# A hybrid block of pooling, gated delta rule and latent attention: four places of the projections' side work

## The chip, the cores and the metric

The kernel runs on one core of one Trainium2 chip. The metric is the device time of one execution in microseconds: the median of three runs of the kernel before is 1230.45 us (1230.11 to 1233.87).

## The reference

One transformer block in float32, 1024 tokens of width 1024. `x` is normalised and projected; the projection is split into a pooling mixer, a gated delta rule (4 heads of 128, chunks) and an attention with latents; their outputs are projected, added to `x`, and a squared-ReLU MLP (1024 to 4096 to 1024) follows.

```python
proj = rms_norm(x, attn_norm) @ w_in
xa, qkv, z, b, a, c_q, c_kv, k_pe = split(proj)
y_a = pool_mixer(xa, ...)                  # windows 2, 4, 8, 16
y_b = gated_deltanet(qkv, z, b, a, ...)    # below
y_c = mla_attention(c_q, c_kv, k_pe, ...)  # latents c_q, c_kv: norm, up-projection, rope, causal softmax
x = x + concat(y_a, y_b, y_c) @ w_out
x = x + square(relu(rms_norm(x, mlp_norm) @ w_up)) @ w_down

# gated_deltanet, per head
q, k, v = split(silu(causal_dwconv(qkv, conv_w)))   # 4 taps
q, k = l2_normalize(q) * D ** -0.5, l2_normalize(k)
a_strict = strict_lower((k * beta) @ k.T * decay)
u, w = solve(I + a_strict, [v * beta, k * beta * exp(gcum)])
attn = lower(q @ k.T * decay)
# scan over the chunks: v_new = u - w @ state; o = q_dec @ state + attn @ v_new;
#                       state = state * g_last + k_dec.T @ v_new
o = rms_norm(o, norm_gain) * silu(z)
```

## The kernel before, in words

Every large product is done in three passes of matmuls on operands split into a high and a low part (`split`, lines 114 to 116: a copy on ScalarE and a subtraction on VectorE or GpSimd; `mm3`, lines 122 to 125). The input projection is made tile by tile: a tile is 128 output channels, and a half tile is 512 tokens of it, 24 matmuls of 512 columns. `proj_tile` (line 479) runs the two halves of one tile. For each half it issues the 24 matmuls into one PSUM bank of the kind `mm` (four of them), calls `use` on the result, then calls what an earlier half tile has left in the list `later`, then `pump(n, m)`, which takes `m` steps of the generators in the queue `slow`, up to two of `ahead` and `n` of those in `side`. After the first half it calls `between`, if there is one.

The order of the tiles is: four key tiles (one per head), two gates, then per head a query tile and a value tile, after the second head two tiles of the pooling mixer, and at the end the other two gates. `conv_silu` (line 498) is the `use` of keys, queries and values: the four taps, the first on ScalarE (line 503), three on VectorE (line 506, reading the PSUM bank, with small pieces on line 508), a Tanh on ScalarE (line 512) and one more VectorE operation (line 514) that stores `kt`, `qt` or a scratch tile. The gates' `use` is a Tanh on ScalarE and the VectorE operation of line 715 that stores `zs`.

Side work that hangs on these tiles:

- `latents()` (line 373), in the queue `slow`: per token tile three steps (`latent_a`: transposes of the latents, up-projection by matmuls, squares), and per pair of token tiles `latent_b` (a Newton iteration of small VectorE operations) and two steps of `latent_c` (fifteen GpSimd operations, one ScalarE operation, a DMA to `n_dram`, line 369). That is 8 steps a pair, 32 for the eight token tiles. During the key tiles `m` is `LAT`, 4; during the gates it is 2.
- For each key head, after its tile: transposes of the keys (line 524), their square sums on ScalarE (line 541), products of the keys with themselves (line 562) and `at` (line 565, VectorE), which goes to `a_dram` (line 566, issued by SyncE) and is read back in another order into `lanes` (line 569).
- After the four key heads: the key scales, a Newton iteration of eleven VectorE operations on 128x32 and one product (lines 576 and 577). They are read on line 705 alone, in `turn_v`.
- `lanes()` (line 580), in the queue `side`: the inverse of 32x32 triangles, one per partition, by 31 steps of two VectorE operations (lines 589 and 591), then a copy of the inverse with its two inner dimensions turned, `TLT` (line 593, VectorE), and two DMAs to `t_dram`: `TL` issued by SyncE, `TLT` by ScalarE.
- `query_key(h)` (line 674): 8 transposes of the query tile, its square sums on ScalarE, 8 products with the keys, and 8 VectorE operations that turn the decay mask `E[h]` into the attention inside a chunk. It is called as `between` of the value tile of the same head, that is behind its first half.
- `turn_v` (line 699): transposes of a half value tile and their scaling; it is left in `later` by one half tile and called behind the matmuls of the next.
- `heads(0, 1)` and `heads(2, 3)` (line 847), in the queue `side`: what builds the whole inverse out of `t_dram` and `a_dram` (`levels`), and the scan over the chunks (`chain`). They begin after the second and after the last head's values.

The order of the instructions on each engine isn't that of the program. A planner orders them before the run: it goes through the program with a model of each instruction's time and lets an engine take, of what it holds to be ready, what stands first in the program. Each engine then runs its list in order. SyncE's list holds most DMAs: the loads of weights (line 447), `n_dram`, `a_dram`, half of the lanes' reads, `TL`.

Of the kernel before, what the change touches and what calls it, by code (L numbers as in the profile page):

```python
# [16 lines left out]
ALU = mybir.AluOpType  # L17
# [13 lines left out]
EPS = 1e-6  # L31
NEG = -1.0e30
DEPTH = 2
LAT = 4
LEAD = 4
AH = 2
LVB = "sm"
# [26 lines left out]
def block_kernel(ctx, tc, x, x_t, params, positions, attn_norm, w_tiles, w_g, w_qb, w_kvb, w_out,  # L64
# [14 lines left out]
    V, A, G, PE = nc.vector, nc.scalar, nc.gpsimd, nc.tensor  # L79
# [12 lines left out]
    def U(shape=(P, 1024), dt=F32, s="u"):  # L92
        return up.tile(list(shape), dt, tag="u", name=nm(s), bufs=YU)
# [7 lines left out]
    def W(shape=(P, 512), dt=F32):  # L101
        return S(shape, "t2k", 5, dt)

    def MM(tag="mm"):
        pool, w = (wide[0], 512) if tag == "mm" else (wide[0], 1024) if tag == "s2" else (ps, 512)
        return pool.tile([P, w], F32, tag=tag, name=nm(tag), bufs=BANKS[tag])
# [15 lines left out]
    def mm3(o, ah, al, bh, bl, first, last):  # L122
        PE.matmul(o, ah, bh, start=first, stop=False)  # L123
        PE.matmul(o, ah, bl, start=False, stop=False)  # L124
        PE.matmul(o, al, bh, start=False, stop=last)  # L125

    def newton_rsqrt(y, v, t):
        yi = y.bitcast(I32)
        V.tensor_scalar(yi, v.bitcast(I32), 1, None, op0=ALU.logical_shift_right)
        V.tensor_scalar(yi, yi, -1, 0x5F3759DF, op0=ALU.mult, op1=ALU.add)  # L130
        for _ in range(3):
            V.tensor_tensor(t, y, y, op=ALU.mult)
            V.scalar_tensor_tensor(t, t, -0.5, v, op0=ALU.mult, op1=ALU.mult)
            V.scalar_tensor_tensor(y, t, 1.5, y, op0=ALU.add, op1=ALU.mult)
# [317 lines left out]
    side, slow, ahead, later = [], [], [], []  # L452
# [10 lines left out]
    def pump(n, m=0, a=AH):  # L463
        step(slow, m)
        step(ahead, a)
        step(side, n)
# [8 lines left out]
    def prefetch(ct):  # L475
        if ct not in loaded:
            loaded[ct] = load_w(w_tiles[ct], eng=V if ct in (15, 2, 10, 3, 11) else G)

    def proj_tile(ct, use, n=0, m=1, halves=(0, 1), tag="mm", between=None):
        prefetch(ct)  # L480
        hi, lo = loaded[ct]
        nxt = tile_order.index(ct) + 1
        for hf in halves:
            if hf == halves[-1] and nxt < len(tile_order):
                prefetch(tile_order[nxt])
            pm = MM(tag)
            due = later[:]
            del later[:]
            for k in range(KD):
                mm3(pm, hi[:, k, :], lo[:, k, :], ht_hi[hf][:, k, :], ht_lo[hf][:, k, :], k == 0, k == KD - 1)  # L490
            use(hf, pm)
            for f in due:
                f()
            pump(n, m)
            if between and hf == halves[0]:
                between()

    def conv_silu(ci, dst, after=None, eng=None):
        carry = C((P, 3), "carry", 4)

        def use(hf, pm):
            acc = W()
            A.activation(acc, pm, AF.Copy, scale=cw[:, ci, 3:4])
            for s in (1, 2, 3):
                w = cw[:, ci, 3 - s:4 - s]
                V.scalar_tensor_tensor(acc[:, s:], pm[:, :512 - s], w, acc[:, s:], op0=ALU.mult, op1=ALU.add)  # L506
                if hf:
                    V.scalar_tensor_tensor(acc[:, :s], carry[:, 3 - s:], w, acc[:, :s], op0=ALU.mult, op1=ALU.add)
            if not hf:
                V.tensor_copy(carry, pm[:, 509:512])  # L510
            th = W()
            A.activation(th, acc, AF.Tanh)
            d = dst(hf) if after else dst[:, hf * 512:(hf + 1) * 512]
            (eng or V).scalar_tensor_tensor(d, th, 1.0, acc, op0=ALU.add, op1=ALU.mult)
            if after:
                after(hf)

        return use

    def transposed(src, use):  # L520
        for b in range(2):
            pt = MM("sm")
            for j in range(4):
                PE.transpose(pt[:, j * P:(j + 1) * P], src[:, (4 * b + j) * P:(4 * b + j + 1) * P], ident)
            use(b, pt)
# [11 lines left out]
    def square_sums(dst):  # L537
        def use(b, pt):
            for j in range(4):
                jk = C((P, 256), "junk", 1, BF16)  # L540
                A.activation(jk[:, 0:P], pt[:, j * P:(j + 1) * P], AF.Square, accum_out=dst[:, 4 * b + j:4 * b + j + 1])
        return use
# [4 lines left out]
    for h in range(H):  # L547
        kt = U(s="kt")
        proj_tile(6 + h, conv_silu(4 + h, kt), 0, LAT)
        KT.append(kt)  # L550
# [22 lines left out]
    skf = sk.rearrange("p a b -> p (a b)")  # L573
    sskf = ssk.rearrange("p a b -> p (a b)")
    rckf = rck.rearrange("p a b -> p (a b)")
    newton_rsqrt(skf, sskf, rckf)
    V.tensor_tensor(skf, skf, sskf, op=ALU.mult)


    def lanes():  # L580
        TL = U((P, 32, 32), s="tl")
        TLT = U((P, 32, 32), s="tlt")
        G.memset(TL.rearrange("p a b -> p (a b)"), 0.0)
        G.affine_select(out=TL, in_=TL, compare_op=ALU.not_equal, fill=1.0, base=0, pattern=[[1, 32], [-1, 32]], channel_multiplier=0)
        tmp = U(s="lt")
        for j in range(31):
            n, m = 31 - j, j + 1
            tv = tmp[:, 512 * (j % 2):512 * (j % 2) + n * m].rearrange("p (a b) -> p a b", a=n)
            V.tensor_tensor(tv, L[:, j, j + 1:32].unsqueeze(2).to_broadcast([P, n, m]),
                            TL[:, j, 0:m].unsqueeze(1).to_broadcast([P, n, m]), op=ALU.mult)  # L590
            V.tensor_tensor(TL[:, j + 1:32, 0:m], TL[:, j + 1:32, 0:m], tv, op=ALU.subtract)
            yield
        V.tensor_copy(TLT, TL.rearrange("p a b -> p b a"))
        nc.sync.dma_start(t_dram[0], TL.rearrange("p a b -> p (a b)"))
        nc.scalar.dma_start(t_dram[1], TLT.rearrange("p a b -> p (a b)"))
        yield

    side.append(lanes())


# [69 lines left out]
    def queries(h, n):  # L670
        qt = QT[h] = U(s="qt")
        proj_tile(2 + h, conv_silu(h, qt), n)

    def query_key(h):
        qt = QT[h]
        transposed(qt, square_sums(ssq[:, h, :]))
        V.tensor_scalar(tq[:, h, :], ssq[:, h, :], EPS, EPS * 128.0, op0=ALU.add, op1=ALU.mult)
        att = E[h]
        for b in range(2):
            pk = MM("sm")  # L680
            for j in range(4):
                c = 4 * b + j
                PE.matmul(pk[:, j * P:(j + 1) * P], KT[h][:, c * P:(c + 1) * P], qt[:, c * P:(c + 1) * P], start=True, stop=True)
            for j in range(4):
                c = 4 * b + j
                V.scalar_tensor_tensor(att[:, c, :], pk[:, j * P:(j + 1) * P], c2[:, h, c:c + 1], att[:, c, :], op0=ALU.mult, op1=ALU.mult)

    def values(h):
        vs = VS[h] = U((P, NC, P), s="vs")
        vt = [None, None]  # L690

        def half(hf):
            vt[hf] = W()
            return vt[hf]

        def use_v(hf):
            later.append(lambda: turn_v(hf))

        def turn_v(hf):
            pt = MM("sm")  # L700
            for j in range(4):
                PE.transpose(pt[:, j * P:(j + 1) * P], vt[hf][:, j * P:(j + 1) * P], ident)
            for j in range(4):
                c = 4 * hf + j
                A.activation(vs[:, c, :], pt[:, j * P:(j + 1) * P], AF.Copy, scale=sk[:, h, c:c + 1])

        return 10 + h, conv_silu(8 + h, half, use_v)

    def gate(h):
        zs = ZS[h] = U(s="zs")  # L710

        def use_z(hf, pm):
            th = W()
            A.activation(th, pm, AF.Tanh, scale=0.5)
            V.scalar_tensor_tensor(zs[:, hf * 512:(hf + 1) * 512], th, 1.0, pm, op0=ALU.add, op1=ALU.mult)  # L715

        return 14 + h, use_z
# [141 lines left out]
    V.tensor_scalar(dn_half, pv("dn_norm"), 0.5, None, op0=ALU.mult)  # L859
    for h in range(2):  # L860
        proj_tile(*gate(h), LANE, 2)
    for h in range(H):
        n = LANE if h < 2 else SIDE
        queries(h, n)
        proj_tile(*values(h), n, between=lambda: query_key(h))
        if h == 1:
            drain()
            side.append(heads(0, 1))
            for i in range(2):
                proj_tile(*mixer(i), SIDE, 3)  # L870
                slow.append(pool(i, XA[i]))
# [413 lines left out]
    n = 0  # L1285
# [11 lines left out]
    n = 0  # L1297
    for q in (3, 2, 1, 0):
        for k in (2 * q, 2 * q + 1):
# [13 lines left out]
            with tc.issue_after(ev.ins), tc.issue_after(sqi.ins):  # L1313
                if n in (3, 4, 5, 6):
                    p = (n - 2) % 4
# [3 lines left out]
                if n in (4, 5, 6, 7):  # L1319
                    p = (n - 3) % 4  # L1320
# [231 lines left out]
```

## Time and profile before

| | |
|---|---|
| median of three runs | 1230.45 us |
| the profiled execution's own time | 1232.37 us |
| its span, first to last instruction | 1230.4 us |
| mean granted clock of TensorE | 0.973 of full speed |
| VectorE busy | 864.9 us (70%) |
| ScalarE busy | 572.1 us (47%) |
| GpSimd busy | 264.4 us (21%) |

The projections with the work beside them take the span from about 60 to 410 us; attention, the output projection and the MLP follow. In the rows below PE is TensorE, DVE VectorE, ACT ScalarE, POOL GpSimd and SP SyncE; "L123" is line 123 of the kernel. A matmul of 512 columns is listed with 0.39 us, but one starts every 0.23 us, since they are pipelined. A row of a timeline gives the start, the duration, the engine, the line, the operation, the tile written and the tiles read, and in brackets how long the engine had been idle before it and what it waited for. The granted clock is given as a share of 2.4 GHz.

### The profile page before, as it was taken

What the parts mean: (1) busy time and instruction counts of PE and PEld (TensorE: products, weight loads), DVE (VectorE), ACT (ScalarE), POOL (GpSimd) and SP (SyncE); (2) the same over time, 40 slices, a digit from 0 to 9 for tenths busy, and PEclk for the clock granted to TensorE, in tenths of its full rate; (3) what the DMA queues carried; (4) which work ended last, traced back from release to release, by engine and by line L of the source; (5) the groups of instructions that cost most, each with busy time, mean ns of one, the idle gap of its engine ahead of it and who ended that gap; (6) DMA issues with size and microseconds to landing.
All of it is one profiled execution on the core that took longest, in us unless ns stands there. A gap on an engine that the chain in (4) does not pass through costs nothing.

```text
span 1230.4 us, 16261 instructions
## 1 busy us (share of the span) xinstructions
PE 1177.7 (96%) x5802; PEld 972.0 (79%) x5802; DVE 864.9 (70%) x1565; ACT 572.1 (47%) x1187; POOL 264.4 (21%) x309
## 2 busy tenths in 40 slices
PE   6999999999999879999899999999999999999998
PEld 5967777787778668788687788888888888888887
DVE  7677649627754878636898767667669897786863
ACT  6555434344554657623364555554554433333330
POOL 0135540142220316300414424324210000000000
PEclk9999999879998989999899999999999999999999
DMA  7102331221021110282224543344369964442202
GB/s 257 57 30 73 124 111 35 85 63 31 32 67 44 48 64 19 94 309 77 86 69 162 188 146 146 145 157 160 146 248 350 354 226 156 137 138 103 99 27 98
DMA packets 85697, 152.61 MB, mean 124 GB/s; under 512 B 25456, under 2 KB 28656, under 8 KB 85616
## 3 DMA queue, kind: packets, MB, share of 16 engines
q1 hardware_dynamic: 76624, 144.23, 33.1%
q10 hardware_dynamic: 8992, 7.34, 1.9%
q8 instruction: 46, 0.75, 0.2%
q14 instruction: 35, 0.29, 0.1%
HBM read 105.41 MB, written 46.14 MB: 123 GB/s over the span
## 4 chain that ended last, share of the span: by engine, by line
PE 75%; DVE 15%; ACT 4%; issue 3%; POOL 2%; DMA 0%; DVEq 0%; ACTq 0%; POOLq 0%
PE mm L1427 14%; PE mm L1183 12%; PE sm L1183 6%; PE ch L1427 5%; PE sm L1427 5%; PE mm L125 5%; PE mm L123 5%; PE mm L124 5%; PE ch L1183 3%; DVE t2k L506 2%; PE sm L756 2%; PE ch L125 1%; DVE wop L116 1%; PE ch L124 1%; PE ch L123 1%
## 5 line engine op out<-in xcount | busy, mean ns | idle before, releaser
L1427 PE MATMUL mm<-dop,dop 128*128 128x512 f32 x768 | 176.1, 389 | 0.0
L1427 PEld LDWEIGHTS mm<-dop,dop 128*128 128x128 f32 x768 | 144.1, 188 | 30.0
L1183 PE MATMUL mm<-H,wop 128*128 128x512 f32 x576 | 139.7, 395 | 3.6 <-DVE uo L1251 2.8
L1183 PEld LDWEIGHTS mm<-H,wop 128*128 128x128 f32 x576 | 108.7, 190 | 28.1 <-DVE uo L1251 4.2
L123 PE MATMUL mm<-H,w 128*128 128x512 f32 x288 | 119.4, 415 | 2.7 <-DVE zs L715 2.7
L115 ACT CAST dop<-wdr 128x1024 fp32r<-128x1024 f32 x48 | 50.4, 1050 | 151.7 <-PE mm L1427 62.9
L125 PE MATMUL mm<-H,w 128*128 128x512 f32 x288 | 118.8, 413 | 0.0
L124 PE MATMUL mm<-H,w 128*128 128x512 f32 x288 | 118.1, 410 | 0.0
L1183 PE MATMUL sm<-op,wop 128*128 128x512 f32 x384 | 92.4, 389 | 1.0 <-ACT p L1249 1.0
L1183 PEld LDWEIGHTS sm<-op,wop 128*128 128x128 f32 x384 | 72.0, 188 | 16.4 <-ACT p L1249 1.5
L116 DVE TENSOR_TENSOR dop<-wdr,dop 128x1024 fp32r<-128x1024 f32 x48 | 58.6, 1220 | 31.2 <-ACT dop L115 31.2
L1273 ACT ACTIVATE uo<-uo 128x512 f32<-128x512 f32 x48 | 30.3, 631 | 98.4 <-DVE uo L1251 57.7
L1220 POOL TENSOR_TENSOR s<-upr 128x512 f32<-128x512 f32 x16 | 24.3, 1519 | 216.1 <-DVE uo L1209 85.9
L1427 PE MATMUL sm<-dop,dop 128*128 128x512 f32 x288 | 67.4, 389 | 0.0
L1427 PE MATMUL ch<-dop,dop 128*128 128x512 f32 x288 | 67.4, 389 | 0.0
L116 POOL TENSOR_TENSOR w<-raw,w 128x1024 fp32r<-128x1024 f32 x13 | 31.9, 2455 | 157.1 <-ACT w L115 153.1
L123 PEld LDWEIGHTS mm<-H,w 128*128 128x128 f32 x288 | 55.8, 194 | 12.1 <-DVE zs L715 3.1
L116 DVE TENSOR_TENSOR wop<-s,wop 128x512 fp32r<-128x512 f32 x64 | 46.2, 737 | 26.2 <-ACT wop L115 26.1
L125 PEld LDWEIGHTS mm<-H,w 128*128 128x128 f32 x288 | 56.3, 195 | 10.2
L124 PEld LDWEIGHTS mm<-H,w 128*128 128x128 f32 x288 | 56.1, 195 | 9.6 <-issue 0.2
L116 DVE TENSOR_TENSOR dop<-H,dop 128x1024 fp32r<-128x1024 f32 x52 | 63.1, 1214 | 0.0
L1427 PEld LDWEIGHTS ch<-dop,dop 128*128 128x128 f32 x288 | 54.1, 188 | 11.2
(390 smaller groups left out, 2654.2 us busy)
## 6 DMA issues: line engine op xcount, KB each, us to landing
H<-u_dram SPq DMA_DIRECT2D x52, 512.0 KB, 4.4
upr<-in_w_up_dram SPq DMA_DIRECT2D x38, 512.0 KB, 4.0
u_dram<-t SPq DMA_DIRECT2D x64, 256.0 KB, 2.0
wdr<-in_w_down_dram SPq DMA_DIRECT2D x32, 512.0 KB, 8.0
u_dram<-uo SPq DMA_DIRECT2D x48, 256.0 KB, 2.0
raw<-in_w_tiles_dram SPq DMA_DIRECT2D x18, 512.0 KB, 3.4
wor<-in_w_out_dram SPq DMA_DIRECT2D x10, 512.0 KB, 8.1
x<-in_x_dram SPq DMA_DIRECT2D x8, 512.0 KB, 3.6
```

The lines of the kernel that those rows point to most:

```text
L115: A.copy(hi, src)
L116: (eng or V).tensor_tensor(lo, src, f32(hi), op=ALU.subtract)
L123: PE.matmul(o, ah, bh, start=first, stop=False)
L124: PE.matmul(o, ah, bl, start=False, stop=False)
L125: PE.matmul(o, al, bh, start=False, stop=last)
L506: V.scalar_tensor_tensor(acc[:, s:], pm[:, :512 - s], w, acc[:, s:], op0=ALU.mult, op1=ALU.add)
L756: PE.matmul(pa[:, c, :], lhs[:, c, :], rhs[:, c, :], start=True, stop=True)
L1183: PE.matmul(o, x_, y_, start=(first and j == 0 and q == 0), stop=(j == 3 and q == 2), skip_group_check=True)
L1220: G.tensor_tensor(v.s12[:, 0], a21, a22, op=ALU.add)
L1273: A.activation(o, o, AF.Relu)
L1427: PE.matmul(o, x_[:, cs_], y_, start=(q in (0, 1, 3) and i == 0 and e == 0), stop=(i == GP - 1 and e == 2), skip_group_check=True)
```

## The change

Four edits, none of which changes what is computed:

- `LAT` is 5 instead of 4, so that the 32 steps of the latents lie in the first seven of the eight half tiles of the keys.
- The key scales become a function that is left in `later` after the first gate tile, and so called behind the matmuls of the second gate's first half, two half tiles after its old place.
- `TLT` is made by `nc.scalar` in place of `nc.vector`.
- `between` of the value tiles leaves `query_key(h)` in `later`, so that it is called behind the matmuls of the second half (after `turn_v` of the first) and no more directly behind the first.

```diff
@@ -31,7 +31,7 @@
 EPS = 1e-6
 NEG = -1.0e30
 DEPTH = 2
-LAT = 4
+LAT = 5
 LEAD = 4
 AH = 2
 LVB = "sm"
@@ -573,8 +573,10 @@
     skf = sk.rearrange("p a b -> p (a b)")
     sskf = ssk.rearrange("p a b -> p (a b)")
     rckf = rck.rearrange("p a b -> p (a b)")
-    newton_rsqrt(skf, sskf, rckf)
-    V.tensor_tensor(skf, skf, sskf, op=ALU.mult)
+
+    def key_scales():
+        newton_rsqrt(skf, sskf, rckf)
+        V.tensor_tensor(skf, skf, sskf, op=ALU.mult)
 
 
     def lanes():
@@ -590,7 +592,7 @@
                             TL[:, j, 0:m].unsqueeze(1).to_broadcast([P, n, m]), op=ALU.mult)
             V.tensor_tensor(TL[:, j + 1:32, 0:m], TL[:, j + 1:32, 0:m], tv, op=ALU.subtract)
             yield
-        V.tensor_copy(TLT, TL.rearrange("p a b -> p b a"))
+        A.copy(TLT, TL.rearrange("p a b -> p b a"))
         nc.sync.dma_start(t_dram[0], TL.rearrange("p a b -> p (a b)"))
         nc.scalar.dma_start(t_dram[1], TLT.rearrange("p a b -> p (a b)"))
         yield
@@ -859,10 +861,12 @@
     V.tensor_scalar(dn_half, pv("dn_norm"), 0.5, None, op0=ALU.mult)
     for h in range(2):
         proj_tile(*gate(h), LANE, 2)
+        if h == 0:
+            later.append(key_scales)
     for h in range(H):
         n = LANE if h < 2 else SIDE
         queries(h, n)
-        proj_tile(*values(h), n, between=lambda: query_key(h))
+        proj_tile(*values(h), n, between=lambda: later.append(lambda: query_key(h)))
         if h == 1:
             drain()
             side.append(heads(0, 1))
```

## Rows read from the trace of the kernel before

**Rows 1.** The page: busy time of TensorE, and the chain that ended last.

```profile
PE 1177.7 (96%) x5802; PEld 972.0 (79%) x5802; DVE 864.9 (70%) x1565; ACT 572.1 (47%) x1187; POOL 264.4 (21%) x309
...
PE 75%; DVE 15%; ACT 4%; issue 3%; POOL 2%; DMA 0%; DVEq 0%; ACTq 0%; POOLq 0%
```

**Rows 2.** Waits of TensorE, 80 to 160 us: awaited, us in total, times, longest.

```profile
PE sm L524 <- DVE kt L514: 1.6, 2, 0.9
PE ch L125 <- DVE lv L116: 1.6, 2, 1.2
```

**Rows 3.** Waits of TensorE, 160 to 240 us.

```profile
PE sm L524 <- DVE qt L514: 3.9, 2, 3.1
PE mm L123 <- DVE zs L715: 2.7, 1, 2.7
```

**Rows 4.** Windows of 2 us: busy by engine, granted clock, DMA share, GB/s.

```profile
170.00:172.00 2.00, 1.32 (x3) 1.13 (x4) 2.00 (x6) 0.00 (x0) 2.00 (x7) 0.64 0.00 0
172.00:174.00 2.00, 2.00 (x6) 1.54 (x6) 1.69 (x3) 0.00 (x0) 2.00 (x4) 0.50 0.00 0
228.00:230.00 2.00, 0.66 (x3) 0.66 (x4) 1.88 (x3) 0.62 (x1) 0.00 (x0) 0.65 0.79 324
230.00:232.00 2.00, 2.00 (x10) 1.72 (x9) 1.22 (x2) 1.48 (x8) 0.00 (x0) 0.50 0.60 217
...
234.00:236.00 2.00, 2.00 (x9) 1.57 (x8) 0.17 (x1) 0.09 (x1) 0.00 (x0) 0.64 0.44 67
```

**Rows 5.** Timeline of VectorE, 160 to 186 us: start, us, instruction, [idle, releaser].

```profile
161.99 0.42 DVE L325 TENSOR_REDUCE ms<-lv 128x4 f32<-128x256 f32 x1 [6.47 <-ACT lv L323]
...
166.13 0.17 DVE L129 TENSOR_SCALAR sk<-ssk 128x32 int32<-128x32 int32 x1
...
169.95 0.67 DVE L715 SCALAR_TENSOR_TENSOR zs<-t2k,mm 128x512 f32<-128x512 f32 x1
...
173.53 0.20 DVE L577 TENSOR_TENSOR sk<-sk,ssk 128x32 f32<-128x32 f32 x1
179.03 2.32 DVE L506 SCALAR_TENSOR_TENSOR t2k<-mm,cw,t2k 128x511 f32<-128x511 f32 x3 [5.30 <-ACT t2k L503]
...
184.35 1.23 DVE L116 TENSOR_TENSOR w<-raw,w 128x1024 fp32r<-128x1024 f32 x1 [2.94 <-ACT w L115]
185.49 0.18 DVE L589 TENSOR_TENSOR lt<-lanes,tl 128x31 f32<-128x31 f32 x1
```

**Rows 6.** Timeline of SyncE's queue, 172 to 180 us.

```profile
173.71 0.34 SPq L369 DMA_DIRECT2D n_dram<-nrm  x1
174.11 0.42 SPq L566 DMA_DIRECT2D a_dram<-at  x1
...
179.17 1.12 SPq L569 DMA_DIRECT2D lanes<-a_dram  x2
```

**Rows 7.** Timeline of GpSimd: starts of the first and last pair.

```profile
91.64 0.40 POOL L348 TENSOR_TENSOR pe<-qk,rs 128x128 f32<-128x128 f32 x1 [5.99 <-DVE rs L134]
...
167.56 0.46 POOL L348 TENSOR_TENSOR pe<-qk,rs 128x128 f32<-128x128 f32 x1 [13.04 <-DVE rck L132]
```

**Rows 8.** Line 503 until 141 us: duration min/median/max, first and last start.

```profile
L503 ACT ACTIVATE t2k<-mm,cw x8: 678/684/698, 73.5 to 139.0; 128x512 f32<-128x512 f32 x8
```

**Rows 9.** Timeline of VectorE, 227 to 230 us.

```profile
227.65 1.03 DVE L593 COPY tlt<-tl 128x1024 f32<-128x1024 f32 x1
228.60 1.29 DVE L514 SCALAR_TENSOR_TENSOR qt<-t2k,t2k 128x512 f32<-128x512 f32 x2
```

**Rows 10.** Timeline of TensorE, 226 to 230 us.

```profile
229.34 0.90 PE L524 MATMUL sm<-ident,qt 128*128 128x128 f32 x3 [3.07 <-DVE qt L514]
```

**Rows 11.** The page's groups: a copy of 1024 columns on ScalarE.

```profile
L115 ACT CAST dop<-wdr 128x1024 fp32r<-128x1024 f32 x48 | 50.4, 1050 | 151.7 <-PE mm L1427 62.9
```

**Rows 12.** Timeline of ScalarE, 228 to 230 us.

```profile
229.38 0.63 ACT L512 ACTIVATE t2k<-t2k 128x512 f32<-128x512 f32 x1 [7.23 <-DVE qt L514]
```

**Rows 13.** Waits of TensorE, 240 to 480 us: line 702.

```profile
PE sm L702 <- DVE t2k L514: 0.5, 1, 0.5
```

## The prediction

> **What bounds the kernel now.** I read the page first, then TensorE's waits by stretch, then the timelines of the engines that it waits for. TensorE is busy for 1177.7 of 1230.4 us [rows 1], so at most 52.7 us of idle time is to be had, and a change that adds and removes no matmul, as this one, can only move that idle time and the clock. The chain that ended last runs through TensorE for 75% and through VectorE for 15% [rows 1]: the places where VectorE is late are where order matters. All that is edited lies between the first key tile and the values of the last head, and there TensorE's waits are few. From 80 to 160 us there are four, 3.2 us in all [rows 2]. From 160 to 240 us there are three, 6.6 us [rows 3]: one of 2.7 us on the first gate's `zs` (call it wait A), and two on a query tile, the longer one 3.1 us (wait B, which ends at 229.34 us [rows 10]), the other 0.8.
>
> Each of the two long waits costs more than itself. In the 4 us after A the granted clock is 0.64 and then 0.50, that is the lower level of 1.2 GHz, and TensorE is busy for 1.32 and 2.00 us [rows 4]. Work done at that clock would have taken 1.32 x 0.36 + 2.00 x 0.50 = 1.5 us less. After B it is 0.66 x 0.35, then twice 2.00 x 0.50 (230 to 234 us, two windows alike) and 2.00 x 0.36 = 2.9 us [rows 4]. So A costs 4.2 us and B 6.0.
>
> Why they are there. VectorE works in order. It sat idle for 6.47 us until 161.99 us, waiting for the squares of the last latent [rows 5], and behind that stood the last key head's `at`, eight of the twelve key-scale operations (from 166.13 us on) and then, at 169.95 us, the first `zs` [rows 5]. That is wait A. The last head's `at` is ready before that `zs`, but SyncE writes it to `a_dram` only at 174.11 us, behind the latents' store to `n_dram` at 173.71, and the lanes are read back from 179.17 us on [rows 6]. So the first lane step runs at 185.49 us, while VectorE has been idle 5.30 us before 179.03 and 2.94 before 184.35 [rows 5]. From 184.35 us VectorE is full: convolutions of queries and values, 62 lane operations, at the end the turned copy `tlt` (1.03 us) and right behind it both halves of the second query [rows 9], for which TensorE waits. That is wait B: the stretch is VectorE's, and its start and length set B.
>
> **The change part by part.**
>
> *The turned copy on ScalarE* takes 1.03 us out of VectorE right in front of the query's two stores [rows 9]: -1.0 us on B's releaser. On ScalarE a copy of as many columns takes 1.05 us [rows 11]; it waits for VectorE's last lane step, and queued behind it is a Tanh of the values that has waited 7.23 us anyway, for VectorE's store of the same query [rows 12]. Its DMA stands on ScalarE's queue as before. So nothing is added; without that cover the cost would be 1.05 us on the Tanh. The Trainium skill speaks against this part: "ScalarE: Activation LUTs", section "Rules for kernel authors", gives plain element-wise work to VectorE rather than ScalarE, since it is faster there. By that rule the -1.0 would be 0 and the sum 1225. The trace has the two durations within 0.02 us of each other, with ScalarE the idle one, and I go by that.
>
> *Key scales* are twelve operations on 128x32, from 166.13 to 173.53 us between others [rows 5]. They go behind the second gate's first half tile, which puts them into VectorE's idle time before 179.03 or 184.35. Eight of them stand before the first `zs`. Several of them fill gaps in another chain, so taking them out brings `zs` forward by 0.5 to 1.1 us; I take 0.7. They issue no DMA. Their only reader scales the values' tile, which is projected four half tiles after the second gate begins, so nobody waits for them.
>
> *Query transposes* (8 transposes, 8 products, 8 ScalarE squares and 9 VectorE operations a head) move behind the next 24 matmuls. In the second head they already ran late, at 229.34 us, because VectorE's stores were late; their place in the program doesn't decide there. For the first head it is the wait of 0.8 us, which lies inside VectorE's stretch: removing it alone only lengthens B, so 0. For the last two heads the nearest row is a wait of 0.5 us on the values' turning [rows 13]. I take 0, with -0.5 as one end and as the other a new wait as long as the longest on such transposes, 3.1 us [rows 3].
>
> *Latents in fewer half tiles.* A pair of token tiles is 8 steps; at 4 steps a half tile it has two half tiles, at 5 it has 1.6. Eight convolutions of the keys begin from 73.5 to 139.0 us [rows 8], one each 9.4 us, so the program asks for a pair every 18.7 us, and now for one every 15.0. What runs is slower: the first pair's turn on GpSimd begins at 91.64 us and the last, three pairs on, at 167.56 [rows 7], 25.3 us a pair. So the setting doesn't pace the latents; it only places them ahead of the keys' convolutions where both are ready. The last pair was asked for in the last two key half tiles, with its end in the first gate, and is now asked for in the fifth to seventh. I take it that the last latent comes at least 2 us sooner (an estimate: a fifth of a half tile's 9.4 us, of up to two half tiles asked for). With the 0.7 of the scales this is the 2.7 us by which `zs` must come forward: wait A goes, -4.2 us. SyncE's stores to `n_dram` (one per token tile) come sooner as well, so up to 4.2 us (from 169.95 to 174.11) in which the write of `at` stood behind one of them can go [rows 5, 6]. On the four waits of the key tiles [rows 2] denser latents can take away the two on `lv` (-1.6) or double all four (+3.2); I take 0, since the number of operations stays.
>
> **Sum.** With A gone TensorE is 4.2 us ahead and so is all that it releases. The full stretch of VectorE begins 4.2 us sooner, at about 180.1 us, with the lanes' data there by then (185.49 less 4.2 is 181.3). It ends 4.2 + 1.0 = 5.2 us sooner. TensorE comes to B 4.2 us sooner, so B shrinks from 3.1 to 2.1 us, and its time at the low clock, taken in proportion, from 2.9 to 1.9. Together -5.2 - 1.0 = -6.2 us. Behind that the kernel keeps its waits, which hang on chains that start when these parts end. The profiled execution took 1232.37 us, 2.0 of it outside its span, so it would become 1226.2. It lies 1.9 us over the median of the three timed runs, and the forecast on their scale is 1230.45 - 6.2 = 1224.2 us.
>
> **Rivals.**
>
> *Nothing moves but the copy and the scales.* For it: 25.3 us a pair against 18.7 asked for says that something else paces the latents. Against it: VectorE's 6.47 us idle on one latent is just what an earlier place can shorten. Then `zs` gains 0.7 us, A's low clock shrinks by 0.4, VectorE's stretch ends 1.1 + 1.0 us sooner, and B's low clock shrinks by 1.0: -3.1 us, 1227.4.
>
> *Both waits go.* If the lanes start early enough to fill the 5.30 and 2.94 us of idle time, VectorE's stretch ends 8.2 + 1.0 us sooner, ahead of TensorE, and B goes with its low clock: -4.2 - 6.0 = -10.2, and the 0.8 of the first head's query as well: 1219.4 us. Against it: the idle time before 179.03 us is spent waiting for a matmul that itself comes sooner, so little of it may be left to fill.
>
> *Slower: a latent's wait in front of the keys.* With more latent steps ahead of the convolutions, VectorE's in-order wait for a latent's squares, 6.47 us long now at a place where only gates stand behind it, can fall among the key tiles, before a convolution that TensorE needs to get its bank back. It decides once the four banks of the projection are full, as they were in A. Then A stays and up to 6.5 us come on top, less 1.0 for the copy: 1236. For it: two of TensorE's four waits there are on a key's store [rows 2]. Against it: neither of them is over 0.9 us, so there is slack.
>
> **How the numbers follow.** Forecast 0.42, nothing moves 0.28, both go 0.18, slower 0.12. A measurement of this kernel can't tell less than about 0.3%, 3.7 us, from no change. Faster by more than that: 0.35 of the forecast, all of the case where both go, and 0.05 of the one where nothing moves (it is 0.6 us short of the bound), 0.58. Slower: 0.11 of its case and 0.02 of the others, where a new wait of 3 us on the keys or on the queries eats the gain and more, 0.13. The same: 0.29. The range is 1216 to 1234 us: below it takes in the case where both go with the 1.6 and the 0.5 on top (1217.3), above it the case where nothing moves with both bounds, 3.2 and 3.1 (1233.7).
>
> **What would show it.** Right: no wait of the projection on `zs` between 160 and 185 us and no low clock after it; the write of `at` to `a_dram` no longer behind an `n_dram` store by 4 us; the first lane step at 182 us or sooner; the copy on ScalarE and the second query's stores directly behind the last lane step; a wait of about 2 us on that query. The step on the latents is wrong if the last pair's turn on GpSimd still begins at 167 us or later. The forecast is wrong if A stands, or if TensorE's waits from 80 to 160 us are over 5 us, or if new waits after 240 us, where I count none, give back what was won.

## The result, and the profile after

The changed kernel is slower: a median of 1241.24 us over four runs (1236.00 to 1244.01) beside 1230.90 us, a ratio of 1.0061 with a 95% interval of 1.0039 to 1.0083, which is 4.8 to 10.2 us. A second measurement of the same kernel gave 1.0083 [1.0060, 1.0106]. The forecast of 1224.2 us and its upper end of 1234 both lie below it. What follows reads the execution of 1236.00 us, the shortest of the four, which has a span of 1234.3 us; beside the 1230.4 of before it shows 3.9 of the 10.3 us between the medians.

The page after: busy time of TensorE and of the others, and the chain that ended last by engine.

```profile
PE 1177.1 (95%) x5802; PEld 970.7 (79%) x5802; DVE 863.9 (70%) x1564; ACT 573.8 (46%) x1188; POOL 262.8 (21%) x309
...
PE 74%; DVE 15%; ACT 4%; issue 3%; POOL 3%; DMA 0%; ACTq 0%; DVEq 0%; POOLq 0%
```

But for one instruction, which has gone over from VectorE to ScalarE, no engine has more to do than in [rows 1]: the same work stands further apart. Where it does, TensorE's waits from 80 to 160 us say (engine, tile, line, awaited; us in total, times, longest):

```profile
PE ch L125 <- DVE lv L116: 2.7, 2, 2.5
PE ch L123 <- ACT lv L115: 2.5, 2, 1.7
PE sm L524 <- DVE kt L514: 2.3, 1, 2.3
PE sm L562 <- ACT junk L541: 0.2, 1, 0.2
```

That is 7.7 us in place of the 3.2 of [rows 2], all of it among the key tiles. From 160 to 240 us, beside the 6.6 us of [rows 3]:

```profile
PE sm L704 <- DVE t2k L514: 4.2, 2, 3.9
PE mm L123 <- DVE zs L717: 1.8, 1, 1.8
```

Wait A has shrunk from 2.7 to 1.8 us but stands; the wait on the query has gone, and one of 3.9 us on the values' transposes is there instead. Two windows of 10 us show the second part of the price, the granted clock:

```profile
90.00:100.00 10.00, 8.34 (x42) 7.29 (x43) 6.87 (x22) 4.76 (x16) 8.14 (x22) 0.83 0.13 53
...
130.00:140.00 10.00, 9.78 (x54) 8.44 (x53) 8.05 (x31) 5.23 (x16) 2.45 (x9) 0.86 0.33 135
```

In the kernel before, the same two have

```profile
90.00:100.00 10.00, 9.52 (x49) 7.36 (x48) 7.84 (x28) 3.28 (x10) 8.20 (x22) 1.00 0.25 102
...
130.00:140.00 10.00, 10.00 (x55) 8.61 (x54) 7.44 (x21) 8.62 (x28) 0.92 (x4) 1.00 0.54 172
```

At 0.83 over 8.34 us and 0.86 over 9.78 TensorE loses 1.4 + 1.4 us more to stretches at its lower level.

The start of a half tile's projection (24 matmuls, counted through the TensorE timeline; half tiles 0 to 7 are keys, 8 to 11 gates, 12 the first query) is the ruler for all that follows, in us (32 and 34 are the first and second half of the third gate):

```
half tile      0       2       4       8      12      20      24      32      34
before      60.03   84.19  102.08  133.26  170.68  221.12  271.70  349.61  365.38
after       59.67   84.29  107.75  142.69  176.93  226.79  280.31  349.54  368.20
```

The changed kernel is level at half tile 2, 5.7 us late at 4, 9.4 late at 8 and 6.2 late at 12. At 4 and 8 it has already done nine more matmuls of the latents' up-projection, so a part of the delay there is work brought forward. At 12 both have done the same, and the 6.2 us are accounted for: from 60 us to that half tile TensorE is idle for 10.0 us in place of 6.6, and takes 106.9 us in place of 104.1 for the same matmuls, which is what the two stretches at the lower clock cost.

At half tile 32 the two kernels are level, at 34 the changed one is 2.8 us late, and at the first matmul of the attention's scores 2.9 (405.58 and 402.69 us). That doesn't undo the loss. The moved transposes shift work behind the start of half tile 32, and the one profile of the kernel before is slow from half tile 20 on: it comes to half tile 34 later than any other kernel here with four latent steps. The better partner is the change without the latents, below.

Two profiles of the changed kernel agree within 0.1 us at the half tiles of the ruler up to 20 (226.79 and 226.83), and within 0.5 at all of them. Behind that the same lists come apart: 1.6 us at half tile 28 (314.29 and 315.89) and 8.3 us at the end of the span (1234.3 and 1242.6). For 560 to 640 us and 700 to 760 us the first profile has

```profile
560.00:640.00 80.00, 74.93 (x323) 60.33 (x322) 63.81 (x104) 32.54 (x55) 15.41 (x10) 0.94 0.23 76
...
700.00:760.00 60.00, 60.00 (x267) 49.67 (x266) 38.18 (x44) 30.43 (x56) 19.56 (x13) 1.00 0.45 163
```

and the second has

```profile
560.00:640.00 80.00, 75.38 (x318) 60.55 (x317) 58.33 (x95) 27.51 (x45) 15.42 (x10) 0.91 0.21 69
...
700.00:760.00 60.00, 59.62 (x257) 49.27 (x258) 39.52 (x44) 32.49 (x59) 19.68 (x12) 0.97 0.42 154
```

So a late part of one profile can't be subtracted from another. I use the ruler for the projections and the ratios for the whole. How the loss at half tile 12 reaches the end, and why the other executions take some 6 us more than the one read here, no run shows.

**Where the first 5.7 us come from.** VectorE, 82 to 92 us, in the changed kernel (start, us, instruction, [idle before, releaser]):

```profile
82.57 0.42 DVE L325 TENSOR_REDUCE ms<-lv 128x4 f32<-128x256 f32 x1 [2.27 <-ACT lv L323]
...
84.79 2.40 DVE L132 TENSOR_TENSOR ts__634<-rs 128x28 f32<-128x28 f32 x1
...
87.67 0.19 DVE L132 TENSOR_TENSOR ts__634<-rs 128x28 f32<-128x28 f32 x1
87.77 0.74 DVE L506 SCALAR_TENSOR_TENSOR t2k<-mm,cw,t2k 128x511 f32<-128x511 f32 x1
...
90.92 0.69 DVE L514 SCALAR_TENSOR_TENSOR kt<-t2k,t2k 128x512 f32<-128x512 f32 x1
```

ScalarE there, the same view:

```profile
81.50 0.48 ACT L316 COPY qk<-ch 128x384 f32<-128x384 f32 x1 [1.65 <-PE ch L125]
82.01 0.53 ACT L323 ACTIVATE lv<-qk 128x384 f32<-128x384 f32 x1
...
83.62 1.05 ACT L115 CAST w<-raw 128x1024 fp32r<-128x1024 f32 x1 [0.16 <-PE mm L124]
84.58 0.68 ACT L503 ACTIVATE t2k<-mm,cw 128x512 f32<-128x512 f32 x1
```

And ScalarE in the kernel before, where the order is the other way round:

```profile
82.11 1.05 ACT L115 CAST w<-raw 128x1024 fp32r<-128x1024 f32 x1 [1.91 <-issue]
83.07 0.68 ACT L503 ACTIVATE t2k<-mm,cw 128x512 f32<-128x512 f32 x1
83.64 0.47 ACT L316 COPY qk<-ch 128x384 f32<-128x384 f32 x1
```

The fifth latent step puts the second token tile's copies and squares (lines 316 to 324) ahead of the key convolution's first tap (line 503), which slips from 83.07 to 84.58. On VectorE the sums of that tile and the first half of the pair's inverse root (lines 325 to 132) stand in front of the other taps, and one of its small operations, two operands of 128x28, lasts 2.40 us beside a split on GpSimd:

```profile
84.75 2.40 POOL L116 TENSOR_TENSOR w<-raw,w 128x1024 fp32r<-128x1024 f32 x1 [7.10 <-ACT w L115]
```

The tap of line 506 begins at 87.77 us (83.78 before), the key's store at 90.92 (88.09 before), and TensorE stands still for it:

```profile
91.66 1.06 PE L524 MATMUL sm<-ident,kt 128*128 128x128 f32 x4 [2.33 <-DVE kt L514]
```

This is the mechanism of the rival "a latent's wait in front of the keys": latent work in front of convolutions that TensorE needs. That rival had a chance of 0.12 and a time of 1236.

### The profile page after: what moved, and what is told of

The parts are those of the page before. It is cut to its first block, busy times and chain, and to the rows that moved or that the text cites. A ratio compares the mean times of both kernels' runs of the same rounds, so it can differ in the third digit from the quotient of the medians.

```text
span 1234.3 us, 16271 instructions
## 1 busy us (share of the span) xinstructions
PE 1177.1 (95%) x5802; PEld 970.7 (79%) x5802; DVE 863.9 (70%) x1564; ACT 573.8 (46%) x1188; POOL 262.8 (21%) x309
## 4 chain that ended last, share of the span: by engine, by line
PE 74%; DVE 15%; ACT 4%; issue 3%; POOL 3%; DMA 0%; ACTq 0%; DVEq 0%; POOLq 0%
PE mm L1431 14%; PE mm L1187 12%; PE sm L1187 6%; PE ch L1431 5%; PE sm L1431 5%; PE mm L124 4%; PE mm L125 4%; PE mm L123 4%; PE ch L1187 3%; DVE t2k L506 2%; PE sm L758 2%; DVE wop L116 1%; PE ch L123 1%; PE ch L125 1%; DVE H L116 1%
## 5 line engine op out<-in xcount | busy, mean ns | idle before, releaser
L116 DVE TENSOR_TENSOR dop<-wdr,dop 128x1024 fp32r<-128x1024 f32 x48 | 58.7, 1222 | 31.3 <-ACT dop L115 31.3
L1431 PEld LDWEIGHTS sm<-dop,dop 128*128 128x128 f32 x288 | 54.1, 188 | 11.2
```

Of the source, the lines that this page charges most:

```text
L116: (eng or V).tensor_tensor(lo, src, f32(hi), op=ALU.subtract)
L1431: PE.matmul(o, x_[:, cs_], y_, start=(q in (0, 1, 3) and i == 0 and e == 0), stop=(i == GP - 1 and e == 2), skip_group_check=True)
```

## Experiments

Ratios are to the kernel before on the same chip, with their 95% intervals.

**Latents alone.** `-LAT = 4` / `+LAT = 5` and nothing else.

> Latents at 5 steps a half tile, the other three parts undone. Theory 1 (the latents now stand in front of the keys' convolutions on VectorE, and TensorE loses some 6 us before the first query tile): slower, 1235 to 1243 us, the first half tile of the first query starts near 177 us instead of 170.7. Theory 2 (the moved query transposes are what costs, by the 4.2 us wait on the values' turning): 1229 to 1232. Theory 3 (no single part costs, only the order that comes out of all four): within 2 us of 1231.

1.0054 [1.0034, 1.0074]; half tile 4 at 109.31 us, half tile 12 at 178.58. The latents alone are as slow as the whole change.

**The change without the latents.** `+LAT = 4`, the three other parts as in the change.

> The copy on ScalarE, the key scales later and the query transposes later, latents at 4 steps as before. Theory 1: not slower than before; by the prediction's own terms without the latents -3.1 us, 1228, TensorE's waits from 60 to 160 us as before (3.5 us). Theory 2: slower, 1234 or more, with the 4 us wait on the values' turning still there. Theory 3: 1229 to 1233.

1.0010 [0.9990, 1.0029]; half tiles 4 and 12 at 101.64 and 170.03 us. The loss before half tile 12 goes with the latents. Beside this kernel, which differs from the changed one in `LAT` alone, the loss also stays: 6.9 us at half tile 12, 8.9 at 24, 6.8 at 32 and 34, and 5.3 at the first attention score (400.28 and 405.58 us). It is so across all kernels measured: the eight profiles with five latent steps behind all or most key half tiles come to that score at 404.91 to 408.65 us, the ten with four or three at 394.13 to 402.69.

**Query transposes alone.** The kernel before with `between=lambda: later.append(lambda: query_key(h))`.

> Query transposes behind the second half of the values' tile, the rest as before. Theory 1: within 2 us of 1231. Theory 2: slower by 3 to 6 us, and TensorE waits on the values' turning near 230 us for about 4 us in place of 3.1 us on the query. Theory 3: within 2 us.

0.9954 [0.9928, 0.9980], median 1229.42 us beside 1232.70: faster than both kernels. A gain that the prediction had at 0, and that the run above, which holds the same move, did not show. Four of its twelve executions took 1220 to 1222 us, the others 1223 to 1233; the profiled one, 1233.24 us, is the longest, so no trace shows how the short ones come about.

**The changed kernel once more**, beside these.

> The changed kernel once more, for the spread of its times and for a second trace. All theories: 1236 to 1244 us, slower than before. If its own trace is over 1238 us, the place where it lies behind the first trace (1236.0) says what varies from run to run; theory 1 and 2 leave that open.

1.0083 [1.0060, 1.0106]: the result repeats.

**Five steps only behind the later key half tiles.** The number of latent steps is 4 behind the first key half tile and 5 behind the seven others.

> The changed kernel, but with 4 latent steps behind the first key half tile and 5 behind the other seven. Theory 1a (the loss is made at the second half tile alone, where a latent's copies stand before the convolution's first tap on ScalarE and a latent's Newton iteration before its other taps on VectorE): TensorE's first query half tile starts near 170.5 us, and the time is that of the kernel with 4 steps throughout, 1231 to 1235. Theory 1b (every later half tile loses some too): it starts between 173 and 176 us, time 1235 to 1240. Theory 3 (the whole order, not this place): near 177 us, 1237 to 1243.

1.0024 [1.0007, 1.0040]; half tile 4 at 102.89, half tile 12 at 173.36 us, 3.6 of the 6.2 us given back. That is theory 1b: the step behind the first half tile costs most, the later ones the rest.

**The copy alone, the scales alone.** `A.copy(TLT, ...)` in one, `later.append(key_scales)` in the other.

> The turned copy on ScalarE alone. The prediction's term: -1.0 us, in any case within 2 us of before. Rival (copy or scales give back what the moved query transposes win, since the three together were no faster than before while the transposes alone were 0.5% faster): if the copy is what gives it back, 2 us or more slower than before.

> The key scales two half tiles later, alone. The prediction's term: -0.7 us, the wait of the projection on the gates near 168 us about 0.7 us shorter. Rival: if the scales are what gives back the transposes' gain, 2 us or more slower than before.

1.0010 [0.9995, 1.0025] and 1.0001 [0.9984, 1.0017]: neither can be told from no change.

**The opposite direction.** Query transposes moved, `LAT = 3`.

> Query transposes moved, and the latents at 3 steps a half tile in place of 4. Theory 1 turned round (fewer latent steps in front of the keys' convolutions help): 1 to 4 us faster than the moved transposes alone (1229), with less waiting of TensorE before 170 us than the 6 us of before. Rival (the latents then end later, and the lanes and the gates wait for them in the same queues): slower than the moved transposes alone, first lane step later than 186 us.

0.9969 [0.9950, 0.9987]; TensorE idle 4.4 us between 60 and 170 us (5.9 before, 8.2 after, 6.2 with the move alone). Neither expectation came true as a whole. The waits shrink, half tile 12 comes at 167.68 us and the first lane step at 170.6, but the whole is no faster than with the move alone (0.9954): five steps cost, and what three win over four, if anything, the ratios can't tell.

**A ring wait?** Behind later key half tiles VectorE and ScalarE wait up to 4.95 us for GpSimd's rotary work (`ro`, line 365), which holds one of three `lv` buffers. The changed kernel with `-rt = C((P, 5, 32), "lv", 3)` / `+rt = C((P, 5, 32), "rt", 2)`:

> The changed kernel whole; the rotary part's product rt gets two buffers of its own instead of one of the three lv buffers. Theory 1b (behind the later key half tiles the fifth latent step stops ScalarE and VectorE at lv buffers that GpSimd's rotary work still holds: waits of 1.9 and 4.4 us in front of the squares and the splits): those waits go, the later key half tiles give back what the ring costs, the first query half tile begins at 173 to 175 instead of 176.9, ratio to before 1.001 to 1.004. Rival (the ring wait only shows who was late; the order of the in-order queues alone costs the time): first query half tile at 176 to 177.5, ratio 1.005 to 1.009.

1.0061 [1.0037, 1.0084], half tile 12 at 177.84 us: the rival. TensorE's waits from 60 to 170 us in this kernel (one of 0.3 us, on the decays, is left out):

```profile
PE ch L125 <- DVE lv L116: 2.6, 2, 2.0
PE ch L308 <- ACT qk L316: 1.3, 1, 1.3
PE sm L524 <- DVE kt L514: 1.0, 1, 1.0
```

There are 2.8 us less of them, the last pair's turn on GpSimd begins at 162.11 us instead of 165.98 and half tile 11 at 165.60 instead of 168.62, yet the first query begins no sooner. The ring was not what set it.

**VectorE beside GpSimd.** First `eng=V if ct in (7, 15, ...)`, meant to take away the split that stands beside the stretched operation:

> The changed kernel whole; the lower half of the split of the second key tile's weights is taken on VectorE instead of GpSimd. Theory 1a-port (the squaring of the inverse root, stretched from 0.19 to 2.40 us beside GpSimd's 2.40 us split, is what makes the first key tile's convolution late): the squaring takes 0.2 us, VectorE pays about 1.2 us for the split, the convolution begins 0.5 to 1.5 us sooner than 87.77, the third projection half tile's successor (half tile 4) begins at 105.5 to 107 instead of 107.75, ratio 1.004 to 1.008. Rival (the order alone, ScalarE's copies and squares of the latent in front of the convolution's silu and the whole inverse root on VectorE): convolution at 87.5 to 89, half tile 4 at 107.5 to 109.5, ratio 1.006 to 1.010.

1.0082 [1.0064, 1.0100], but a miss: the split at 84.7 us is that of tile 8, so the stretch of 2.40 us stood, and the run says nothing on it. Then `eng=V if ct in (8, 15, ...)`:

> The changed kernel whole; the lower half of the split of the third key tile's weights on VectorE instead of GpSimd. If VectorE's squaring beside GpSimd's split makes the first key convolution late: no operation of the inverse root over 0.6 us near 84.8, the convolution begins 1 to 2.2 us sooner than 87.77 unless VectorE takes its own 1.2 us for the split before it, half tile 4 starts at 105.5 to 107 instead of 107.75, ratio 1.003 to 1.006. Rival (the order of the lists alone): half tile 4 at 107.5 to 109.5, ratio 1.005 to 1.009.

VectorE in this kernel:

```profile
84.72 0.19 DVE L132 TENSOR_TENSOR ts__634<-rs 128x28 f32<-128x28 f32 x1
84.83 1.23 DVE L116 TENSOR_TENSOR w<-raw,w 128x1024 fp32r<-128x1024 f32 x1
85.98 0.74 DVE L506 SCALAR_TENSOR_TENSOR t2k<-mm,cw,t2k 128x511 f32<-128x511 f32 x1
```

The stretch is gone (0.19 us), the tap begins 1.8 us sooner, half tile 4 at 104.86 us instead of 107.75. So the stretch is real and half of the loss there. But half tile 12 begins at 177.42 us and the ratio is 1.0069 [1.0046, 1.0092]: of what is won at the first key 4.4 us are left at half tile 11 (164.23 instead of 168.62), and they are waited for again at the last key. The same edit on moved transposes and later scales:

> The kernel before with moved transposes and later scales (0.9960), and the third key tile's split on VectorE. If the stretch costs there too (one small piece, 1.0 us): ratio 0.993 to 0.996. If VectorE's 1.2 us for the split costs more than the stretch: 0.996 to 0.999.

0.9976 [0.9958, 0.9995]; without the edit 0.9960 (below), intervals that overlap: nothing gained.

**Which part takes the transposes' gain?** The kernel before with the move and the copy, and with the move and the scales:

> The kernel before with the query transposes moved and the turned copy on ScalarE, key scales and latents as before. The move alone gave 0.9954, with the copy and the scales together 1.0010. If the copy on ScalarE gives the gain back (it stands there in front of work that heads 2 and 3 or the values wait for): ratio 0.999 to 1.002. If not: 0.994 to 0.998.

> The kernel before with the query transposes moved and the key scales two half tiles later, copy and latents as before. If the later scales give the transposes' gain back (they fall into the stretch of VectorE in which the first query tile is worked): ratio 0.999 to 1.002. If not: 0.994 to 0.998. If neither this run nor the one with the copy loses the gain, it is their sum or the spread of the kernel with the move alone that stands behind 1.0010.

1.0010 [0.9995, 1.0026] with the copy, 0.9960 [0.9940, 0.9980] with the scales. It is the copy. TensorE with the move alone, around its wait for the values' transposes:

```profile
227.76 0.39 PE L124 MATMUL mm<-H,w 128*128 128x512 f32 x1
231.21 0.66 PE L702 MATMUL sm<-ident,t2k 128*128 128x128 f32 x4 [3.07 <-DVE t2k L514]
```

With the copy as well:

```profile
226.11 0.39 PE L124 MATMUL mm<-H,w 128*128 128x512 f32 x1
230.42 0.66 PE L702 MATMUL sm<-ident,t2k 128*128 128x128 f32 x4 [3.92 <-DVE t2k L514]
```

With the copy, the transposes stand six matmuls earlier in TensorE's list, presumably because the planner now holds VectorE to be done sooner. VectorE does deliver 0.79 us sooner, but six matmuls at the 0.227 us between two of them are 1.36 us, so TensorE waits longer with less done. Half tile 22 begins at 241.48 instead of 240.12 us and half tile 24 at 271.69 instead of 268.27; part of that is the clock from 260 to 270 us, with the move alone

```profile
260.00:270.00 10.00, 10.00 (x67) 9.13 (x65) 4.32 (x9) 4.14 (x9) 4.37 (x5) 0.67 0.13 53
```

and with the copy

```profile
260.00:270.00 10.00, 10.00 (x61) 8.87 (x60) 3.51 (x7) 2.17 (x4) 3.20 (x4) 0.55 0.13 53
```

**Does it add up in the changed kernel?** The changed kernel with `V.tensor_copy(TLT, ...)`:

> The changed kernel with the turned copy back on VectorE: moved transposes, later scales, five latent steps. If the costs add (latents alone 1.0054, transposes with scales 0.9960): ratio 1.000 to 1.003, TensorE's wait in front of the values' transposes 3.1 instead of 3.9 us, first attention score 2 to 5 us sooner than the 405.6 of the changed kernel. If the latents' delay swallows the transposes' gain whatever the copy does: ratio 1.005 to 1.008.

1.0065 [1.0041, 1.0089]: it does not. The wait before the values' transposes falls to 2.4 us, but half tile 12 is at 178.49 us, as with the latents alone (178.58), and the first attention score at 406.87 (407.01 there). The 3.1 us between them at half tile 32 (349.31 against 352.38) are no gain: with the move, the last head's query transposes and products stand behind that start, not before it, and at half tile 34 the two are level (367.98 and 368.13). All kernels with the move take 2.9 us longer than the others from half tile 32 to 34, whatever `LAT` is. With five latent steps the moved transposes gain nothing, whatever the copy does.

**A version out of all this.** Transposes, scales, `LAT = 3`:

> The kernel before with moved transposes, later scales, copy on VectorE and three latent steps behind a half tile instead of four. With four steps the first two gave 0.9960; moved transposes with three steps alone 0.9969 and a TensorE idle of 4.4 instead of 6.2 us between 60 and 170. If fewer steps give time and the transposes' gain stays: ratio 0.992 to 0.996. If fewer steps only make the last latents late and that is paid at the first lane step or in front of the scores: 0.995 to 0.999.

0.9958 [0.9940, 0.9976], median 1229.12 us. It, the move alone (0.9954) and the move with the scales (0.9960) beat both kernels and can't be told apart.

## Why the prediction was wrong

*The failed step is the term for the four waits of the key tiles: "I take 0, since the number of operations stays".* The number stayed, the order did not. The four waits of 3.2 us became 7.7, more than the upper bound of doubling, and two stretches at the lower clock came with them. The latents alone give 1.0054, the whole change without them 1.0010. I had the mechanism as a rival but let it "decide once the four banks of the projection are full"; it decided with the first convolution, where TensorE waited for the transposes of a late `kt`, not for a bank.

*"The last latent comes at least 2 us sooner ... `zs` must come forward."* The first half came about, the second did not follow. GpSimd's last pair:

```profile
165.98 0.40 POOL L348 TENSOR_TENSOR pe<-qk,rs 128x128 f32<-128x128 f32 x1 [12.52 <-DVE rs L134]
```

That is 1.6 us before the 167.56 of [rows 7], and on VectorE the sums of the last latent begin 4.6 us sooner, at 157.40 us in place of 161.99 [rows 5]. But VectorE, 148 to 177 us:

```profile
148.66 0.56 DVE L116 TENSOR_TENSOR lv<-ch,lv 128x384 fp32r<-128x384 f32 x1 [4.95 <-POOL ro L365]
...
157.40 0.42 DVE L325 TENSOR_REDUCE ms<-lv 128x4 f32<-128x256 f32 x1 [1.21 <-ACT lv L323]
...
163.15 0.69 DVE L514 SCALAR_TENSOR_TENSOR kt<-t2k,t2k 128x512 f32<-128x512 f32 x1
...
169.71 0.51 DVE L552 TENSOR_SCALAR ssk<-ssk 128x8 f32<-128x8 f32 x1 [3.88 <-ACT junk L541]
...
175.16 1.13 DVE L565 SCALAR_TENSOR_TENSOR at<-sm,c,E 128x128 f32<-128x128 f32 x4 [2.67 <-PE sm L562]
176.20 1.28 DVE L717 SCALAR_TENSOR_TENSOR zs<-t2k,mm 128x512 f32<-128x512 f32 x2
```

In [rows 5] a latent was what VectorE waited for before the first `zs`. With the latents ahead, the last key head has taken their place: its `kt` is stored at 163.15 us (149.32 before), its `at` at 175.16, and `zs` comes at 176.20, 6.2 us later than before, not 2.7 sooner. I had asked only what would release `zs` if the latent came sooner, and not what the latent overtakes. That wait A "goes, -4.2" fell with it.

What the second half of `at` waits for is TensorE. In its list the last eight products of the key stand behind all the matmuls of the second gate. In VectorE's list `zs` stands behind `at`, and the first query needs the bank that `zs` reads:

```profile
174.07 1.05 PE L562 MATMUL sm<-kt 128*128 128x128 f32 x8
176.93 0.67 PE L123 MATMUL mm<-H,w 128*128 128x512 f32 x1 [1.81 <-DVE zs L717]
```

In the kernel before they come some 9.5 us sooner:

```profile
164.52 1.16 PE L562 MATMUL sm<-kt 128*128 128x128 f32 x8
```

The kernel without the ring wait and the one with the third split on VectorE have these products in the same place, at 173.13 and 173.37 us, and `zs` at 177.11 and 176.69. There each gives back what it had won up to half tile 11.

*"The write of `at` ... behind the latents' store"* came out in its small part. SyncE in the changed kernel:

```profile
171.69 4.35 SPq L369 DMA_DIRECT2D n_dram<-nrm  x2
176.31 0.32 SPq L566 DMA_DIRECT2D a_dram<-at  x1
```

The write follows `at` (175.16 and 1.13 us) at once instead of standing behind a store, but it is still 2.2 us later than that of [rows 6], since `at` is late. The first lane step follows at 187.28 us (185.49 before), not at 182 or sooner.

*The copy, -1.0 on VectorE and nothing on ScalarE.* ScalarE in the changed kernel:

```profile
232.79 1.98 ACT L595 COPY tlt<-tl 128x1024 f32<-128x1024 f32 x1 [4.97 <-DVE tl L593]
```

It took 1.98 us, not the 1.05 of [rows 11]; that row is a cast of columns that lie side by side, and this copy reads a turned view. That the view makes the difference is likely, but no run has a plain copy beside it. The Trainium skill's rule that I argued away ("ScalarE: Activation LUTs", section "Rules for kernel authors") gives `relu`, `max`, `min`, `add` and `mul` to VectorE, with a figure for bf16. It doesn't name a float32 copy, but the trace points the same way: 1.98 us against the 1.03 of [rows 9]. The second query did follow the last lane step directly, as the prediction said, at 232.62 us; the wait was simply not that query's any more. The copy alone gained nothing, and next to the moved transposes it lost their gain.

*The scales, `zs` 0.7 us sooner.* They hardly moved. In the run with the later scales alone VectorE still takes seven of the twelve operations, in place of eight, ahead of the first `zs`:

```profile
165.56 0.17 DVE L129 TENSOR_SCALAR sk<-ssk 128x32 int32<-128x32 int32 x1
...
166.99 0.19 DVE L133 SCALAR_TENSOR_TENSOR rck<-rck,ssk 128x32 f32<-128x32 f32 x1
...
169.17 1.27 DVE L717 SCALAR_TENSOR_TENSOR zs<-t2k,mm 128x512 f32<-128x512 f32 x2
```

They are ready there and VectorE has gaps, so they fill the gaps as before, wherever the program has them. Wait A is 2.5 instead of 2.7 us, so 0.2 us of the 0.7, which the ratio of 1.0001 can't see.

*The transposes, 0 with -0.5 as the lower end.* Alone they give -0.46% [-0.72%, -0.20%], some 5.7 us, far outside that end. I had reasoned that "their place in the program doesn't decide", since their `qt` was late anyway. It does: with the move TensorE finds other matmuls before it waits, and half tile 21 begins at 226.17 instead of 231.96 us. A wait of 3.07 us on the values' turning takes the query's place, and the moved work follows, so that 2.1 us are left at half tile 22 (240.12 and 242.24). This error was in the cautious direction and is hidden in the changed kernel.

*What stays open.* With five steps the last products of the key hold the first query half tile at 177 to 178 us; why the planner puts them behind the gates' matmuls, the runs don't show. The ring and the stretch were taken away one at a time, not together. A change in the planner's order alone, with the set of steps kept, was not tried. Nor is it settled why the moved transposes gain with four latent steps and not with five.

## What to carry to other kernels

When side work is put further ahead in in-order lists, count what it overtakes on each engine, not only what it releases; an engine's total staying equal says nothing. After a moved step, ask what the next latest releaser is, and price a moved instruction by a row with its own access pattern. See whether a step that was moved in the program has moved on its engine: work that is ready early still fills the early gaps. And compare starts only at points before which both kernels have done the same work. Try the parts of a change alone: here one part gained 0.46%, one lost 0.54%, and the sum showed only the loss.

## Of the hardware

An operation of VectorE with two operands of 128x28 lasted 2.40 us beside a 2.40 us operation of GpSimd, and 0.19 us once that was moved away. The Trainium skill's page "SBUF — State Buffer", section "Terms", has the two engines share a pair of ports that one holds for a whole instruction; the pair of runs agrees. That two profiles of one and the same program can lie 8.3 us apart, with the granted clock lower in some late stretches of one, I had not expected either; what decides it, no run here tells.
